# Strided attention on one core: normalisation spread over three engines, sums one group ahead, and stores of half the partitions

## The chip, the cores and the metric

The kernel runs on one core of a Trainium2 chip. The metric is the device time of one execution in microseconds (us). Seven executions of the kernel before gave a median of 129.85 us (129.51 to 129.98).

## What is computed

Attention in which every query looks at the same few keys: of the 1024 positions, those at 0, 64, 128, ..., 16 in all. Batch 8, heads 12, sequence 1024, head dimension 64, all float32.

```python
attend_positions = np.arange(0, seq, stride)
k = K[:, :, attend_positions, :]
v = V[:, :, attend_positions, :]
scores = np.einsum('bhqd,bhkd->bhqk', q, k) / np.sqrt(dim)
weights = np.exp(scores - np.max(scores, axis=-1, keepdims=True))
weights = weights / (np.sum(weights, axis=-1, keepdims=True) + 1e-10)
result[:, :, i, :] = np.einsum('bhqk,bhkd->bhqd', weights, v)[:, :, 0, :]
```

The output has the shape of Q. Q is 25.2 MB and so is the output; of K and V only one row in 64 is read.

## The kernel before

The 96 pairs of batch and head are taken in 24 groups of 4 (`HG`, `NG`). A group's queries fill one SBUF tile of 128 partitions by 2048 float32 numbers, 1 MB: each partition holds 32 consecutive rows of one head. In the output tile of a group a partition holds 16 consecutive rows of one head, and 16 of the head two further on. All DMAs are issued by SyncE (SP) on one queue, in the order of the program; each also waits until the eighth DMA before it on that queue has landed.

At the start K, V and the first ten groups of Q are loaded (`QBUFS = 10`), and constants are made: an identity, two permutations of it, a selector of the four heads (`s_sel`, and `slot_m` as float32), a mask for the values. `keys(m)` multiplies the keys of eight groups with the four head masks (L161, VectorE), spreads them with products on TensorE (L169) into a PSUM tile from the pool of the outputs, and copies them into `k_t` (L177, ScalarE). `value_rows` casts V and spreads it into `v_rep` by four products (L188) and four casts (L192).

A group then goes through these steps:

- `cast`: float32 to bfloat16 on GpSimd (L207)
- `transpose`: 32 by 32 blocks on VectorE (L211)
- `scores`: four accumulating products on TensorE into one PSUM bank (L218), then exp on ScalarE in two halves of 64 partitions (L229), into one of three weight tiles
- `values`: the value rows times the mask on GpSimd (L199)
- `sums`: eight small products with `s_sel` (L238), and a reciprocal on VectorE (L242)
- `outputs(g, c)` for c from 0 to 3: two products into a PSUM tile of one bank (L249), and the scaling with the reciprocals on VectorE (L254), into `out_sb`
- `store`: 1 MB to DRAM; a partition's 8 KB go out as two runs of 4 KB

The order on each engine is that of the program, since the schedule is written by hand (`manual_schedule`). In round g of the loop stand, in this order, the transpose of group g + 2, the sums of g, half of the outputs of g, the scores of g + 1, the other half of the outputs, the values of g + 2, the cast of g + 3, the store of g, and the load of g + 10. `keys` for later groups stands in rounds 2 and 4.

The output tiles are nine (`OBUFS = 9`), the PSUM pool of the outputs has four tiles of one bank.

Of the kernel before, what the change touches and what calls it, by code (L numbers as in the profile page):

```python
# [11 lines left out]
FP32 = mybir.dt.float32  # L12
BF16 = mybir.dt.bfloat16
I16 = mybir.dt.int16
I32 = mybir.dt.int32
AF = mybir.ActivationFunctionType
ALU = mybir.AluOpType


def _ap_with(ap: bass.AP, new_ap, extra_offset: int = 0) -> bass.AP:  # L20
    return dataclasses.replace(
        ap, ap=[list(p) for p in new_ap], offset=ap.offset + extra_offset
    )


def _copy(nc, out: bass.AP, in_: bass.AP):

    sides = [
        mybir.BassSymbolicTensorAccessPattern(
            ap=side.ap, dtype=side.dtype, bass_ap=side,  # L30
            is_dma=True, for_custom_bir_dma=True,
        )
        for side in (in_, out)
    ]
    return nc.sync.add_instruction(
        mybir.InstDMACopy(
            name=nc.get_next_instruction_name(), engine=mybir.EngineType.SP,
            ins=sides[:1], outs=sides[1:], queue="qSPDynamicHW",
            mode="Copy",
        )  # L40
    )
# [4 lines left out]

@with_exitstack
def kernel(  # L50
    ctx: ExitStack,
# [7 lines left out]
    nc = tc.nc  # L59

    B, H, S, D = Q.shape
    NK = S // stride
    scale = 1.0 / math.sqrt(D)

    P = 128
    HG = 4
    NG = B * H // HG
    NC = NG // 2
    SD = S * D
    KW = P + NK  # L70
    assert B * H == NG * HG and S == 1024 and D == 64 and NK == 16
    QBUFS = 10
    OBUFS = 9

    const = ctx.enter_context(tc.tile_pool(name="const", bufs=1))
    qn_pool = ctx.enter_context(tc.tile_pool(name="qn", bufs=QBUFS))
    out_pool = ctx.enter_context(tc.tile_pool(name="outsb", bufs=OBUFS))
# [2 lines left out]
    vb_pool = ctx.enter_context(tc.tile_pool(name="vb", bufs=3))  # L80
    rec_pool = ctx.enter_context(tc.tile_pool(name="rec", bufs=2))
    psum_sc = ctx.enter_context(tc.tile_pool(name="psc", bufs=2, space=bass.MemoryType.PSUM))
    psum_o = ctx.enter_context(tc.tile_pool(name="po", bufs=4, space=bass.MemoryType.PSUM))
    psum_s = ctx.enter_context(tc.tile_pool(name="psm", bufs=2, space=bass.MemoryType.PSUM))

    ctx.enter_context(tc.manual_schedule())
# [3 lines left out]
    v_raw = const.tile([P, NC, D], FP32, name="v_raw")  # L90
# [3 lines left out]
    def load(g):  # L94
        qn[g] = qn_pool.tile([P, 32 * D], FP32, name="qn", tag="qn")
        n = P if g < 2 else 32
        _copy(nc, qn[g], _ap_with(Q, [[HG * SD // n, n], [1, HG * SD // n]], g * HG * SD))
# [14 lines left out]
    perm_v = const.tile([P, 2, 2, 2, 2, NK], BF16, name="perm_v")  # L112
# [8 lines left out]
    for c in range(2):  # L121
        for a in range(2):
            for e in range(2):
                nc.gpsimd.tensor_copy(
                    out=perm_v[:, c, a, :, e], in_=id_v[:, c, :, a]
# [5 lines left out]
    for i in range(3):  # L131
# [7 lines left out]
        out=slot_i, in0=iota_p, scalar1=4, scalar2=3,  # L139
# [4 lines left out]
    s_sel = const.tile([P, 4], BF16, name="s_sel")  # L144
    nc.vector.tensor_scalar(  # L145
        out=s_sel, in0=col4, scalar1=slot_f, scalar2=None, op0=ALU.is_equal
    )
    slot_m = const.tile([P, 4], FP32, name="slot_m")
    nc.vector.tensor_copy(out=slot_m, in_=s_sel)
    mask = const.tile([P, 4, D], BF16, name="mask")  # L150
# [4 lines left out]
    v_rep = const.tile([P, NC, 2, D], BF16, name="v_rep")  # L155


    def keys(m):
        kr = k_raw[:, 4 * m : 4 * m + 4].rearrange("p n (q f) -> p n f q", f=2)
        for h in range(4):  # L160
            nc.vector.tensor_scalar(  # L161
                out=k_m[:, 4 * m : 4 * m + 4, :, h], in0=kr,
                scalar1=slot_m[:, h : h + 1], scalar2=None, op0=ALU.mult,
            )
        for u in range(2):
            kp = psum_o.tile([P, 2, 2, 2, 4 * NK], FP32, name="kp", tag="o")
            for i in range(2):
                for f in range(2):
                    nc.tensor.matmul(  # L169
                        kp[:, i, :, f],  # L170
                        lhsT=k_m[:, 4 * m + 2 * u + i, f].rearrange("p h q -> p (h q)"),
                        rhs=perm_k.rearrange("p c a b k -> p c (a b k)"),
                        start=True, stop=True,
                    )
            g0 = 8 * m + 4 * u
            dst = k_t[:, g0 : g0 + 4]
            nc.scalar.copy(  # L177
                _ap_with(dst, [dst.ap[0], [KW, 8], [32, 4], [1, NK]], extra_offset=NK),
                kp.rearrange("p i c f (s k) -> p (i c f) s k", s=4),
            )  # L180


    def value_rows():
        nc.vector.tensor_copy(out=v_bf, in_=v_raw)
        for n in range(2):
            for c in range(2):
                vp = psum_sc.tile([P, NC // 2, D], FP32, name="vp", tag="sc")
                nc.tensor.matmul(  # L188
                    vp, lhsT=perm_v[:, c].rearrange("p a b e k -> p (a b e k)"),
                    rhs=v_bf[:, 6 * n : 6 * n + 6], start=True, stop=True,  # L190
                )
                nc.vector.tensor_copy(out=v_rep[:, 6 * n : 6 * n + 6, c], in_=vp)  # L192

    qb, qt, wt, vb, rec, out_sb = {}, {}, {}, {}, {}, {}


    def values(g):
# [7 lines left out]
    def cast(g):  # L205
        qb[g] = qb_pool.tile([P, 32 * D], BF16, name="qb", tag="qb")
        nc.gpsimd.tensor_copy(out=qb[g], in_=qn[g])  # L207

    def transpose(g):
        qt[g] = qt_pool.tile([P, 32 * D], BF16, name="qt", tag="qt")  # L210
        nc.vector.transpose(qt[g].bitcast(I32), qb[g].bitcast(I32))  # L211

    def scores(g):
        sc = psum_sc.tile([P, 512], FP32, name="sc", tag="sc")
        q = qt[g]
        for e in range(2):
            for f in range(2):
                nc.tensor.matmul(  # L218
                    sc, lhsT=k_t[:, g, f, NK * (1 - e) : NK * (1 - e) + P],
                    rhs=_ap_with(  # L220
                        q, [q.ap[0], [2 * D, 8], [16 * D, 2], [2, 32]],
                        extra_offset=D * e + f,
                    ),
                    start=e + f == 0, stop=e + f == 2,
                )
        w = wt[g] = w_bufs[g % 3]
        for a in range(2):
            wa = w[64 * a : 64 * a + 64]
            nc.scalar.activation(  # L229
                out=_ap_with(wa, [wa.ap[0], [P, 8], [1, 2], [2, 32]], extra_offset=64 * a),  # L230
                in_=sc[64 * a : 64 * a + 64].rearrange("p (t x q) -> p t x q", t=8, x=2),
                func=AF.Exp, bias=0.0, scale=scale,
            )

    def sums(g):
        sm = psum_s.tile([P, 2, 8, 2], FP32, name="sm", tag="sm")
        for i in range(8):
            nc.tensor.matmul(  # L238
                sm[:, :, i], lhsT=wt[g][:, i], rhs=s_sel, start=True, stop=True
            )  # L240
        rec[g] = rec_pool.tile([P, 2, 16], FP32, name="rec", tag="rec")
        nc.vector.reciprocal(rec[g], sm.rearrange("p b i e -> p b (i e)"))  # L242

    def outputs(g, c):
        if c == 0:
            out_sb[g] = out_pool.tile([P, 2, 16, D], FP32, name="out_sb", tag="out_sb")
        ps = psum_o.tile([P, 2, 2, 2 * D], FP32, name="o_ps", tag="o")
        for i in range(2):
            nc.tensor.matmul(  # L249
                ps[:, :, i], lhsT=wt[g][:, 2 * c + i],  # L250
                rhs=vb[g].rearrange("p s d -> p (s d)"),
                start=True, stop=True,
            )
        nc.vector.tensor_tensor(  # L254
            out=out_sb[g][:, :, 4 * c : 4 * c + 4],
            in0=ps.rearrange("p b i (e d) -> p b (i e) d", e=2),
            in1=rec[g][:, :, 4 * c : 4 * c + 4].unsqueeze(3).to_broadcast([P, 2, 4, D]),
            op=ALU.mult,
        )

    def store(g):
        o = out_sb[g]
        _copy(
            nc,
            _ap_with(out, [[16 * D, P], [2 * SD, 2], [1, 16 * D]], g * HG * SD),
            _ap_with(o, [o.ap[0], [1, 1], [1, 32 * D]]),
        )

    keys(0)
    cast(0)  # L270
    transpose(0)
    scores(0)
    value_rows()
    values(0)
    cast(1)
    transpose(1)
    values(1)
    cast(2)
    for g in range(NG):
        if g + 2 < NG:  # L280
            transpose(g + 2)
        sums(g)
        outputs(g, 0)
        outputs(g, 1)
        if g + 1 < NG:
            scores(g + 1)
        outputs(g, 2)
        outputs(g, 3)
        if g + 2 < NG:
            values(g + 2)  # L290
        if g + 3 < NG:
            cast(g + 3)
        if g in (2, 4):
            keys(g // 2)
        store(g)
        if g + QBUFS < NG:
            load(g + QBUFS)


# [1 line left out]
_INS = ['Q', 'K', 'V', 'stride']  # L301
_OUTS = [((8, 12, 1024, 64), 'float32')]
# [30 lines left out]
```

The softmax here doesn't subtract the row's maximum and nothing guards it: scores larger than these inputs give would overflow.

## Time and profile before

One execution was profiled:

| What | Value |
|---|---|
| Time of the profiled execution | 129.78 us |
| Its span, first to last instruction | 128.0 us |
| VectorE (DVE) busy | 109.2 us, 85% |
| GpSimd (POOL) busy | 66.6 us, 52% |
| TensorE (PE) busy | 74.4 us, 58% |
| ScalarE (ACT) busy | 39.6 us, 31% |
| Mean DMA rate over the span | 400 GB/s |
| First store issued | 23.57 us |
| Second store issued | 27.55 us |
| Last store issued | 120.1 us |

The profile is read so: a slice is a fortieth of the span, and a digit in it is the busy share in tenths. A group of instructions has its busy time, its count and the mean time of one. The DMA share is the mean busy share of the sixteen DMA engines of the core. Durations of one instruction can overlap with the next on the same engine: a run of four L254 takes 2.48 us where one has 0.68.

### The profile page before, as it was taken

How to read it: one execution, taken by the hardware profiler on the slowest of the kernel's cores; microseconds unless marked ns; L12 is line 12 of the kernel's file. 1: busy time of each engine (PE TensorE's matmuls, PEld its weight loads, DVE VectorE, ACT ScalarE, POOL GpSimd, SP SyncE). 2: the span in 40 equal slices, each digit the busy share in tenths (PEclk: the TensorE clock that was granted, in tenths of full speed). 3: DMA queues.
4: the chain of work that ended last, by engine and by line, in shares of the span. 5: the costliest groups of instructions: out<-in, count | busy, mean ns of one | idle time of the engine just before them, and what ended most of it. 6: DMA issues, size and time to landing. Idle time of an engine off the chain costs nothing. (4 is left out here: it accounts for less than half of the span.)

```text
span 128.0 us, 1518 instructions
## 1 busy us (share of the span) xinstructions
PE 74.4 (58%) x508; PEld 39.2 (31%) x508; DVE 109.2 (85%) x170; ACT 39.6 (31%) x55; POOL 66.6 (52%) x69
## 2 busy tenths in 40 slices
PE   0007767974486097866675579776567579674000
PEld 0003233441433064333342234333334333332000
DVE  6996458999969986899999999999999999999500
ACT  3003404224234234344423440444442343432000
POOL 8971499675217605387767644738765743100000
PEclk9999999999769855599999965579999955999655
DMA  2999989898998998989989999999999999999980
GB/s 69 356 315 479 461 369 481 369 451 351 479 458 343 494 404 379 509 366 415 499 335 448 433 402 440 438 397 448 438 394 453 402 425 420 422 425 422 425 353 41
DMA packets 7913, 51.23 MB, mean 400 GB/s; under 512 B 3872, under 2 KB 3872, under 8 KB 3872
## 3 DMA queue, kind: packets, MB, share of 16 engines
q1 hardware_dynamic: 7904, 51.12, 96.4%
q8 instruction: 4, 0.07, 0.2%
q14 instruction: 5, 0.04, 0.1%
HBM read 25.95 MB, written 25.17 MB: 399 GB/s over the span
## 5 line engine op out<-in xcount | busy, mean ns | idle before, releaser
L254 DVE TENSOR_TENSOR out_sb<-o_ps,rec 128x512 f32<-128x512 f32 x96 | 59.9, 684 | 5.0 <-PE o_ps L249 2.7
L229 ACT ACTIVATE w<-sc 64x512 bf16<-64x512 f32 x48 | 35.1, 731 | 60.3 <-PE sc L218 57.5
L207 POOL CAST qb<-qn 128x2048 bf16<-128x2048 f32 x24 | 45.5, 1897 | 0.9 <-DMA qn<-in_Q_dram 0.9
L249 PE MATMUL o_ps<-vb,w 128*128 128x256 bf16 x192 | 38.1, 327 | 1.8 <-DVE out_sb L254 1.0
L199 POOL TENSOR_TENSOR vb<-mask,v_rep 128x256 bf16<-128x256 bf16 x24 | 16.1, 669 | 41.1 <-PE o_ps L249 36.8
L218 PE MATMUL sc<-qt,k_t 128*128 128x512 bf16 x96 | 33.9, 487 | 1.4 <-DVE qt L211 1.2
L211 DVE STREAM_TRANSPOSE qt<-qb 128x1024 int32<-128x1024 int32 x24 | 29.6, 1235 | 1.6 <-POOL qb L207 1.6
L249 PEld LDWEIGHTS <-w 128*128 128x128 bf16 x192 | 19.7, 112 | 15.6 <-issue 8.2
L238 PE MATMUL sm<-s_sel,w 128*128 128x4 bf16 x192 | 8.7, 167 | 21.8 <-ACT w L229 21.8
L238 PEld LDWEIGHTS <-w 128*128 128x128 bf16 x192 | 7.0, 101 | 29.9 <-ACT w L229 29.3
L218 PEld LDWEIGHTS <-k_t 128*128 128x128 bf16 x96 | 11.1, 117 | 12.4 <-issue 7.1
L169 PE MATMUL kp<-perm_k,k_m 128*128 128x128 bf16 x24 | 3.1, 311 | 17.4 <-DVE k_m L161 17.4
L242 DVE RECIPROCAL rec<-sm 128x32 f32<-128x32 f32 x24 | 7.8, 326 | 0.3 <-PE sm L238 0.3
L169 PEld LDWEIGHTS <-k_m 128*128 128x128 bf16 x24 | 2.3, 140 | 18.2 <-DVE k_m L161 18.2
L177 ACT CAST k_t<-kp 128x512 bf16<-128x512 f32 x6 | 3.2, 589 | 14.1 <-PE kp L169 14.1
L161 DVE TENSOR_SCALAR k_m<-k_raw,slot_m 128x256 bf16<-128x256 f32 x12 | 6.8, 626 | 0.0
L192 DVE CAST v_rep<-vp 128x384 bf16<-128x384 f32 x4 | 2.2, 558 | 2.6 <-PE vp L188 2.6
L135 POOL MEMSET k_t<- 128x4608 bf16 x1 | 3.9, 3940 | 0.0
L145 DVE TENSOR_SCALAR s_sel<-col,slot_f 128x4 bf16<-128x4 int16 x1 | 3.1, 3145 | 0.1
L188 PE MATMUL vp<-v_bf,perm_v 128*128 128x384 bf16 x4 | 2.0, 489 | 0.8 <-DVE v_rep L192 0.6
L177 ACT ACT_TABLE_LOAD x1 | 1.3, 1283 | 2.1 <-DVE k_t L129 2.1
L129 DVE MEMSET k_t<- 128x1152 uint32 x1 | 1.0, 1018 | 1.0 <-PEq L314 1.0
(17 smaller groups left out, 6.2 us busy)
## 6 DMA issues: line engine op xcount, KB each, us to landing
qn<-in_Q_dram SPq DMA_DIRECT2D x24, 1024.0 KB, 13.8
out_dram<-out_sb SPq DMA_DIRECT2D x24, 1024.0 KB, 11.9
k_raw<-in_K_dram SPq DMA_DIRECT2D x1, 384.0 KB, 4.5
v_raw<-in_V_dram SPq DMA_DIRECT2D x1, 384.0 KB, 7.6
```

Of the source, the lines that this page charges most:

```text
L161: nc.vector.tensor_scalar(out=k_m[:, 4 * m : 4 * m + 4, :, h], in0=kr, scalar1=slot_m[:, h : h + 1], scalar2=None, op0=ALU.mult,)
L169: nc.tensor.matmul(kp[:, i, :, f], lhsT=k_m[:, 4 * m + 2 * u + i, f].rearrange("p h q -> p (h q)"), rhs=perm_k.rearrange("p c a b k -> p c ...
L177: nc.scalar.copy(_ap_with(dst, [dst.ap[0], [KW, 8], [32, 4], [1, NK]], extra_offset=NK), kp.rearrange("p i c f (s k) -> p (i c f) s k", s=4),)
L199: nc.gpsimd.tensor_tensor(out=vb[g], in0=mask, in1=v_rep[:, g // 2, g % 2].unsqueeze(1).to_broadcast([P, 4, D]), op=ALU.mult,)
L207: nc.gpsimd.tensor_copy(out=qb[g], in_=qn[g])
L211: nc.vector.transpose(qt[g].bitcast(I32), qb[g].bitcast(I32))
L218: nc.tensor.matmul(sc, lhsT=k_t[:, g, f, NK * (1 - e) : NK * (1 - e) + P], rhs=_ap_with(q, [q.ap[0], [2 * D, 8], [16 * D, 2], [2, 32]], ex ...
L229: nc.scalar.activation(out=_ap_with(wa, [wa.ap[0], [P, 8], [1, 2], [2, 32]], extra_offset=64 * a), in_=sc[64 * a : 64 * a + 64].rearrange( ...
L238: nc.tensor.matmul(sm[:, :, i], lhsT=wt[g][:, i], rhs=s_sel, start=True, stop=True)
L242: nc.vector.reciprocal(rec[g], sm.rearrange("p b i e -> p b (i e)"))
L249: nc.tensor.matmul(ps[:, :, i], lhsT=wt[g][:, 2 * c + i], rhs=vb[g].rearrange("p s d -> p (s d)"), start=True, stop=True,)
L254: nc.vector.tensor_tensor(out=out_sb[g][:, :, 4 * c : 4 * c + 4], in0=ps.rearrange("p b i (e d) -> p b (i e) d", e=2), in1=rec[g][:, :, 4 ...
```

## The change

The steps of a group are the same, but they are cut and ordered differently.

- `OBUFS` goes from 9 tiles of one group (8 KB in a partition) to 4 tiles of two groups (16 KB). The PSUM pool of the outputs goes from four tiles of one bank to two of two banks.
- `keys` is split. `key_rows` does the masking, on ScalarE in place of VectorE, in rounds 1 and 5; the products and copies follow in rounds 2 and 6, into PSUM tiles of the scores.
- `value_rows` is split in two, the second half in round 3, into PSUM tiles of the sums. The cast of V stands alone before the scores of group 0.
- The casts of groups 0 and 1 stand at the start; the transpose of group 1 follows the scores of group 0.
- The query positions of a group are laid out in another order (the access pattern in `scores`), so that a head's rows lie together in the output tile.
- `sums` is split. `sums_mm` forms the sums with the selector as the stationary side and the weights as the moving side, four products of 32 rows; `sums_rec` transposes them from PSUM in 32 by 32 blocks and takes reciprocals. Both are done for group g + 1 in round g.
- `outputs` keeps only products, four into one PSUM tile; `normalize` scales. Of the two halves, the first is scaled by VectorE in one instruction of 1024 elements; of the second, VectorE scales 512 elements, and the other 512 are copied by ScalarE and scaled in SBUF by GpSimd.
- The scores of g + 1 come before all outputs of g.
- `store(n, h)` stores half the partitions (64) of two groups, 16 KB a partition in four runs of 4 KB. After every second group two such stores are issued, each followed by a load.

```diff
-    OBUFS = 9
+    OBUFS = 4
...
-    psum_o = ctx.enter_context(tc.tile_pool(name="po", bufs=4, space=bass.MemoryType.PSUM))
+    psum_o = ctx.enter_context(tc.tile_pool(name="po", bufs=2, space=bass.MemoryType.PSUM))
...
+    sel32 = const.tile([P, 32], BF16, name="sel32")
+    nc.vector.memset(sel32, 0.0)
+    nc.vector.tensor_copy(out=sel32[:, 0:4], in_=s_sel)
...
-    def keys(m):
+    def key_rows(m):
         kr = k_raw[:, 4 * m : 4 * m + 4].rearrange("p n (q f) -> p n f q", f=2)
         for h in range(4):
-            nc.vector.tensor_scalar(
-                out=k_m[:, 4 * m : 4 * m + 4, :, h], in0=kr,
-                scalar1=slot_m[:, h : h + 1], scalar2=None, op0=ALU.mult,
-            )
+            nc.scalar.activation(
+                out=k_m[:, 4 * m : 4 * m + 4, :, h], in_=kr,
+                func=AF.Copy, scale=slot_m[:, h : h + 1],
+            )
+
+    def keys(m):
         for u in range(2):
-            kp = psum_o.tile([P, 2, 2, 2, 4 * NK], FP32, name="kp", tag="o")
+            kp = psum_sc.tile([P, 2, 2, 2, 4 * NK], FP32, name="kp", tag="sc")
...
-    def value_rows():
-        nc.vector.tensor_copy(out=v_bf, in_=v_raw)
-        for n in range(2):
-            for c in range(2):
-                vp = psum_sc.tile([P, NC // 2, D], FP32, name="vp", tag="sc")
+    def value_rows(n):
+        for c in range(2):
+            vp = psum_s.tile([P, NC // 2, D], FP32, name="vp", tag="sm")
...
-                        q, [q.ap[0], [2 * D, 8], [16 * D, 2], [2, 32]],
-                        extra_offset=D * e + f,
+                        q, [q.ap[0], [D, 8], [16 * D, 2], [2, 32]],
+                        extra_offset=8 * D * e + f,
...
-    def sums(g):
-        sm = psum_s.tile([P, 2, 8, 2], FP32, name="sm", tag="sm")
-        for i in range(8):
+    def sums_mm(g):
+        sm = sm_ps[g] = psum_s.tile([P, 8, 32], FP32, name="sm", tag="sm")
+        for q in range(4):
             nc.tensor.matmul(
-                sm[:, :, i], lhsT=wt[g][:, i], rhs=s_sel, start=True, stop=True
-            )
-        rec[g] = rec_pool.tile([P, 2, 16], FP32, name="rec", tag="rec")
-        nc.vector.reciprocal(rec[g], sm.rearrange("p b i e -> p b (i e)"))
+                sm[32 * q : 32 * q + 32], lhsT=sel32,
+                rhs=wt[g][:, :, 32 * q : 32 * q + 32],
+                start=True, stop=True, tile_position=(0, 32 * q),
+            )
+
+    def sums_rec(g):
+        sm = sm_ps[g]
+        smt = rec_pool.tile([P, 8, 32], FP32, name="smt", tag="smt")
+        nc.vector.transpose(
+            smt.rearrange("p i r -> p (i r)"), sm.rearrange("p i r -> p (i r)")
+        )
+        rec[g] = rec_pool.tile([P, 8, 4], FP32, name="rec", tag="rec")
+        nc.vector.reciprocal(rec[g], smt[:, :, 0:4])
 
     def outputs(g, c):
         if c == 0:
-            out_sb[g] = out_pool.tile([P, 2, 16, D], FP32, name="out_sb", tag="out_sb")
-        ps = psum_o.tile([P, 2, 2, 2 * D], FP32, name="o_ps", tag="o")
-        for i in range(2):
+            if g % 2 == 0:
+                out_2[g // 2] = out_pool.tile(
+                    [P, 2, 4, 8, D], FP32, name="out_sb", tag="out_sb"
+                )
+            out_sb[g] = out_2[g // 2][:, g % 2]
+        ps = psum_o.tile([P, 4, 4, D], FP32, name="o_ps", tag="o")
+        o_ps[g, c] = ps
+        for i in range(4):
             nc.tensor.matmul(
-                ps[:, :, i], lhsT=wt[g][:, 2 * c + i],
+                ps[:, i].rearrange("p s d -> p (s d)"), lhsT=wt[g][:, 4 * c + i],
                 rhs=vb[g].rearrange("p s d -> p (s d)"),
                 start=True, stop=True,
             )
+
+    def normalize(g, c):
+        ps = o_ps[g, c]
+        i0 = 4 * c
+        n = 4 if c == 0 else 2
+        part = lambda k, m: out_sb[g][:, :, k : k + m].rearrange("p s i d -> p i s d")
+        fact = lambda k, m: rec[g][:, k : k + m].unsqueeze(3).to_broadcast([P, m, 4, D])
+        if n < 4:
+            nc.scalar.copy(part(i0 + n, 4 - n), ps[:, n:4])
         nc.vector.tensor_tensor(
-            out=out_sb[g][:, :, 4 * c : 4 * c + 4],
-            in0=ps.rearrange("p b i (e d) -> p b (i e) d", e=2),
-            in1=rec[g][:, :, 4 * c : 4 * c + 4].unsqueeze(3).to_broadcast([P, 2, 4, D]),
-            op=ALU.mult,
-        )
-
-    def store(g):
-        o = out_sb[g]
+            out=part(i0, n), in0=ps[:, 0:n], in1=fact(i0, n), op=ALU.mult
+        )
+        if n < 4:
+            nc.gpsimd.tensor_tensor(
+                out=part(i0 + n, 4 - n), in0=part(i0 + n, 4 - n),
+                in1=fact(i0 + n, 4 - n), op=ALU.mult,
+            )
+
+    def store(n, h):
+        o = out_2[n][64 * h : 64 * h + 64]
         _copy(
             nc,
-            _ap_with(out, [[16 * D, P], [2 * SD, 2], [1, 16 * D]], g * HG * SD),
-            _ap_with(o, [o.ap[0], [1, 1], [1, 32 * D]]),
-        )
-
+            _ap_with(
+                out, [[16 * D, 64], [2 * SD, 4], [1, 16 * D]],
+                2 * n * HG * SD + h * SD,
+            ),
+            _ap_with(o, [o.ap[0], [1, 1], [1, 64 * D]]),
+        )
+
+    key_rows(0)
+    cast(0)
+    cast(1)
+    transpose(0)
     keys(0)
-    cast(0)
-    transpose(0)
+    nc.vector.tensor_copy(out=v_bf, in_=v_raw)
     scores(0)
-    value_rows()
+    transpose(1)
+    value_rows(0)
     values(0)
-    cast(1)
-    transpose(1)
     values(1)
     cast(2)
+    sums_mm(0)
+    sums_rec(0)
     for g in range(NG):
         if g + 2 < NG:
             transpose(g + 2)
-        sums(g)
+        if g + 1 < NG:
+            scores(g + 1)
         outputs(g, 0)
         outputs(g, 1)
         if g + 1 < NG:
-            scores(g + 1)
-        outputs(g, 2)
-        outputs(g, 3)
+            sums_mm(g + 1)
         if g + 2 < NG:
             values(g + 2)
         if g + 3 < NG:
             cast(g + 3)
-        if g in (2, 4):
-            keys(g // 2)
-        store(g)
-        if g + QBUFS < NG:
-            load(g + QBUFS)
+        normalize(g, 0)
+        normalize(g, 1)
+        if g + 1 < NG:
+            sums_rec(g + 1)
+        if g in (1, 5):
+            key_rows(g // 4 + 1)
+        if g in (2, 6):
+            keys(g // 4 + 1)
+        if g == 3:
+            value_rows(1)
+        if g % 2 == 1:
+            for h in range(2):
+                store(g // 2, h)
+                if g - 1 + h + QBUFS < NG:
+                    load(g - 1 + h + QBUFS)
```

## The prediction

> **What bounds the kernel now.** I read the page's slices first, then its queue table, its chain, its groups, and then asked for the busy time in stretches.
>
> From the page, parts 2 to 4 and 6:
>
> ```profile
> DMA  2999989898998998989989999999999999999980
> q1 hardware_dynamic: 7904, 51.12, 96.4%
> HBM read 25.95 MB, written 25.17 MB: 399 GB/s over the span
> ...
> DVE out_sb L254 1%; DVEq L328 0%; DVE rec L242 0%
> ...
> qn<-in_Q_dram SPq DMA_DIRECT2D x24, 1024.0 KB, 13.8
> out_dram<-out_sb SPq DMA_DIRECT2D x24, 1024.0 KB, 11.9
> ```
>
> The DMA digits stand at 8 or 9 from the second slice to the last but one, and the packets took 96.4% of sixteen engines' span: 123.4 of 128.0 us. The chain names VectorE, but holds only a few per cent of the span, so it doesn't say what bounds. A transfer of 1 MB lands 12 to 14 us after its issue, five times the 2.5 us that 1.05 MB needs at 425 GB/s: transfers stand in line.
>
> From the busy time by stretch (stretch, length, busy us and instructions of PE, PEld, DVE, ACT, POOL, then clock, DMA share, GB/s):
>
> ```profile
> 0.00:4.00 4.00, 0.00 (x0) 0.00 (x0) 2.64 (x6) 1.28 (x1) 3.40 (x21) 1.00 0.42 98
> 12.00:20.00 8.00, 5.98 (x25) 2.27 (x24) 3.98 (x6) 1.47 (x3) 5.54 (x6) 1.00 1.05 442
> 20.00:28.00 8.00, 6.53 (x39) 3.30 (x38) 7.79 (x13) 2.94 (x4) 6.71 (x6) 1.00 0.95 397
> ...
> 56.00:84.00 28.00, 19.46 (x142) 10.30 (x141) 27.34 (x44) 10.23 (x14) 18.05 (x15) 0.83 1.03 434
> ...
> 112.00:120.00 8.00, 3.69 (x36) 2.17 (x36) 7.82 (x14) 2.05 (x3) 0.00 (x0) 0.94 1.01 422
> 120.00:124.00 4.00, 0.00 (x0) 0.00 (x0) 0.11 (x1) 0.00 (x0) 0.00 (x0) 0.50 0.99 416
> 124.00:126.00 2.00, 0.00 (x0) 0.00 (x0) 0.00 (x0) 0.00 (x0) 0.00 (x0) 0.50 0.34 143
> ```
>
> The DMA engines are full from 4 to 124 us, at about 425 GB/s, with loads alone, with both kinds, and with stores alone after 104. VectorE is nearly full too (27.34 of 28 us) but ends at 120.1, with some 4 us of transfers left. So the bound is bytes over DMA rate: 51.12 MB at 425 GB/s is 120 us, after a start of 3 and before a tail of 4. VectorE is second by about 2 us.
>
> The groups that the change touches:
>
> ```profile
> L254 DVE TENSOR_TENSOR out_sb<-o_ps,rec 128x512 f32<-128x512 f32 x96 | 59.9, 684 | 5.0 <-PE o_ps L249 2.7
> L229 ACT ACTIVATE w<-sc 64x512 bf16<-64x512 f32 x48 | 35.1, 731 | 60.3 <-PE sc L218 57.5
> L207 POOL CAST qb<-qn 128x2048 bf16<-128x2048 f32 x24 | 45.5, 1897 | 0.9 <-DMA qn<-in_Q_dram 0.9
> L199 POOL TENSOR_TENSOR vb<-mask,v_rep 128x256 bf16<-128x256 bf16 x24 | 16.1, 669 | 41.1 <-PE o_ps L249 36.8
> L211 DVE STREAM_TRANSPOSE qt<-qb 128x1024 int32<-128x1024 int32 x24 | 29.6, 1235 | 1.6 <-POOL qb L207 1.6
> L242 DVE RECIPROCAL rec<-sm 128x32 f32<-128x32 f32 x24 | 7.8, 326 | 0.3 <-PE sm L238 0.3
> L177 ACT CAST k_t<-kp 128x512 bf16<-128x512 f32 x6 | 3.2, 589 | 14.1 <-PE kp L169 14.1
> L161 DVE TENSOR_SCALAR k_m<-k_raw,slot_m 128x256 bf16<-128x256 f32 x12 | 6.8, 626 | 0.0
> ```
>
> [...]
>
> **The change part by part.**
>
> *Scaling on three engines, sums by transpose.* Before, VectorE has per group 1235 + 4 × 684 + 326 = 4.30 us by durations; back to back it runs a group in about 3.97 (15.64 busy in 16 us holds four). After: transpose 1235; one scaling of 1024 elements, estimated from 512 at 684 ns and a slope of 1 ns an element, 1.19; one of 512, 684; a transpose of 256 from PSUM, estimated from 1235 less 768 elements, 0.47; reciprocal 326. Sum 3.91, so 0.39 less: a pitch near 3.6. GpSimd gets 512 elements of float32:[...] L199's 669 for half as many gives 1.3; I take 1.2. Its group becomes 1.90 + 0.67 + 1.2 = 3.8. ScalarE: 2 × 731 and a copy of 512 near 589, 2.1. No engine passes the DMA's pace, 2.1 MB a group or 4.9 us. Gain on the time: nothing, since the transfers cover it; without that cover it would be 24 × 0.39 = 9 us.
>
> *Key masks to ScalarE, key products in the score banks, values in two steps.* VectorE loses 12 × 626 = 7.5 us (two runs of 2.8 lie in the loop), ScalarE gains 12 of 0.4 to 0.7 us and has 60 us of idle time. In the loop keys now wait for a score bank, 1 to 2 us twice; again beside transfers. Nothing either way.
>
> *Early second cast and transpose.* Groups 0 and 1 end earlier: the cast of group 1 no longer stands behind the value product (at 15.07 us before, after a wait of 4.4). The first store leaves later than now (23.57), as it needs both groups; I put it at 26 to 27, about where group 1's store is now (27.55). The ten first loads are 11.3 MB with keys and values; summing the stretches they keep the engines to 30 us or so. So no hole, unless the first pair is later than 29; each us beyond that would cost one.
>
> *Sums one group ahead.* The sums now wait for exp of g+1 on TensorE; behind them stand the scores of g+2, which the next sums need. A round is 1.9 of scores, 1.7 of exp beside outputs, 0.5 of sums: about 4.1, under 4.9.
>
> *The stores.* Same 24, same 1.05 MB, but each from 64 partitions of 16 KB where it was 128 of 8 KB. Per-packet cost can fall: between nothing and 1 us in all. [...] The tail between 124 and 126 us at a share of 0.34 shows that engines do finish apart, by some 2 us of 120. [...] 24 × 2.1 = 51 us. All of it lies on the path, since nothing else sets the end.
>
> Sum against the profiled execution: 129.78 (128.0 of span) + 51 = 181; it stands 0.07 below the median 129.85.
>
> **The rivals.**
>
> A (forecast): [...] 172 to 188, likeliest 181. For: the bound is DMA, nothing covers it. Against: no half-width transfer is in this trace.
>
> B: [...] engines drift apart, as the tail hints; penalty 10 to 42 us, 140 to 172, about 157.
>
> C, the other side: the half-width stores run at full rate[...]. Then bytes are the same, the larger packets save up to 1 us, no hole opens: 129.0, range 128.6 to 129.6. Decisive point: a store costs no more than 2.46 us of the engines' time. That VectorE's saving shows as 9 us is excluded by the DMA share.
>
> D: stores are full rate, but the new hand-offs between engines bring a group's round to 4.5 us, so the last pair leaves at 27 + 22 × 4.5 = 126 and its 2 MB land 7 us later: 133 to 136. Up to 4.2 us a round it would not show. For: exp, sums, their transpose, the copy on ScalarE and the scaling on GpSimd now follow each other across engines within a round; against: the sums for TensorE and GpSimd above.
>
> **How the numbers follow.** A 0.53, B 0.24, C 0.17, D 0.06. The time is A's, 181. The range leaves out C and what is above A: 131 to 189; A's own is 172 to 188. A measurement here can tell about 0.2%, 0.26 us, from no change. Faster takes most of C, 0.15; within 0.2% the rest of it, 0.02; slower 0.83.
>
> **What would show it.** If A: DMA digits still 9, but GB/s near 290 where loads and stores mix (2.1 MB in 2.46 + 4.6 us) and near 225 where only stores are left; 4.6 us between landings of stores; compute idle, waiting for free output tiles. If B, the rate climbs along the run. If C: over 420 GB/s throughout and a first store before 29 us. If D: DMA digits under 9 after the first third. VectorE's row for 1024 elements near 1.2 us, GpSimd's scaling near 1.2, and a VectorE share well under 85% would bear out the compute sums. I am wrong altogether if the rate of stores alone is above 400 GB/s.

## The result and the profile after

The changed kernel took 137.77 us (median of 12 runs), the kernel before 129.82. Its own runs lie between 134.2 and 143.3: the three nearest its fastest (134.2 to 135.4), which alone count for the ratio, are 3.8% slower than the kernel before (1.038, 95% interval 1.035 to 1.041), the medians differ by 6.1%, and the execution that was profiled is among the slower ones. It took 138.7 us, 136.6 of them in the span.

From its page, parts 2 to 4 and 6:

```profile
span 136.6 us, 1401 instructions
...
DMA  3999899989899998999999999999999999999950
...
q1 hardware_dynamic: 6368, 51.12, 95.3%
...
HBM read 25.95 MB, written 25.17 MB: 374 GB/s over the span
...
DMA 54%; POOL 14%; issue 8%; DVE 6%; PE 3%; SPq 3%; DVEq 1%; ACT 0%; POOLq 0%
...
qn<-in_Q_dram SPq DMA_DIRECT2D x24, 1024.0 KB, 19.7
out_dram<-out_sb SPq DMA_DIRECT2D x24, 1024.0 KB, 19.6
```

The DMA engines are as full as before, with the same 51.12 MB in fewer packets, yet they move 374 GB/s where it was 399. The chain of waits now follows transfers: half of the span is the wait for them. A busy digit here says that packets are under way, not that they go at full speed: below, a share of 1.00 goes with 367 GB/s.

The busy time by stretch says when the speed was missing (stretch, length, busy us and instructions of PE, PEld, DVE, ACT, POOL, then clock, DMA share, GB/s):

```profile
20.00:32.00 12.00, 8.81 (x57) 4.42 (x58) 11.76 (x17) 8.82 (x15) 12.00 (x11) 1.00 0.95 397
32.00:56.00 24.00, 19.13 (x111) 9.42 (x111) 22.21 (x33) 15.12 (x25) 21.51 (x20) 0.93 1.00 367
56.00:84.00 28.00, 17.98 (x92) 8.51 (x91) 20.30 (x30) 12.24 (x18) 17.68 (x16) 0.75 1.00 403
84.00:100.00 16.00, 10.77 (x49) 5.00 (x49) 11.36 (x17) 6.18 (x9) 10.92 (x10) 0.71 1.00 426
112.00:120.00 8.00, 5.57 (x29) 2.63 (x28) 6.15 (x9) 2.77 (x5) 4.70 (x5) 0.63 1.01 408
120.00:128.00 8.00, 0.00 (x0) 0.00 (x0) 1.96 (x3) 0.59 (x1) 1.04 (x1) 0.58 1.01 343
128.00:136.00 8.00, 0.00 (x0) 0.00 (x0) 0.00 (x0) 0.00 (x0) 0.00 (x0) 0.50 0.45 170
```

Before the first store moves at about 30 us nothing is different (393 GB/s from 20 to 28 us, 397 before). The rate drops with the first stores, climbs for 50 us by itself, is whole between 84 and 100, and drops again at the end. In the kernel before, the stretch of the drop ran at 427 GB/s, at a DMA share of 1.01:

```profile
32.00:56.00 24.00, 15.99 (x111) 9.21 (x112) 20.54 (x34) 7.99 (x12) 10.15 (x9) 0.72 1.01 427
```

The trace shows something else beside the rate, from the signals with which each of the sixteen engines reports its part of a transfer. They finish a transfer within 0.5 us of each other at 31 us, within 3 us at 45, within 9.4 us from 91 to 111. They drift apart as the rate recovers. A packet of 16 KB took 0.61 to 0.62 us when undisturbed and up to 1.5 in the slow stretches; a load's packet of 32 KB up to 2.5 instead of 1.21.

The new operations, by shape:

```profile
L282 DVE TENSOR_TENSOR out_sb<-o_ps,rec 128x1024 f32<-128x1024 f32 x24 | 28.6, 1190 | 1.4 <-PE o_ps L268 0.9 <-DVE rec L255 0.5
L286 POOL TENSOR_TENSOR out_sb<-out_sb,rec 128x512 f32<-128x512 f32 x24 | 25.0, 1042 | 6.5 <-ACT out_sb L281 6.5
L282 DVE TENSOR_TENSOR out_sb<-o_ps,rec 128x512 f32<-128x512 f32 x24 | 16.2, 676 | 0.4 <-ACT out_sb L281 0.3
L281 ACT COPY out_sb<-o_ps 128x512 f32<-128x512 f32 x24 | 14.1, 586 | 9.3 <-DMA out_dram<-out_sb 6.9 <-PE o_ps L268 1.7 <-issue 0.2
```

They cost about what was estimated. Of the 9.3 us that ScalarE stood idle before its copies, 6.9 were waits for output tiles whose stores hadn't landed.

### The profile page after: what moved, and what is told of

The parts are those of the page before. It is cut to its first block, busy times and chain, and to the rows that moved or that the text cites. A ratio compares the mean times of both kernels' runs of the same rounds, so it can differ in the third digit from the quotient of the medians.

```text
span 136.6 us, 1401 instructions
## 1 busy us (share of the span) xinstructions
PE 78.8 (58%) x412; PEld 37.5 (27%) x412; DVE 95.3 (70%) x136; ACT 58.8 (43%) x91; POOL 90.5 (66%) x93
## 3 DMA queue, kind: packets, MB, share of 16 engines
q1 hardware_dynamic: 6368, 51.12, 95.3%
## 4 chain that ended last, share of the span: by engine, by line
DMA 54%; POOL 14%; issue 8%; DVE 6%; PE 3%; SPq 3%; DVEq 1%; ACT 0%; POOLq 0%
DMA out_dram<-out_sb 47%; DMA qn<-in_Q_dram 7%; POOL qb L211 6%; POOL out_sb L286 5%; POOL vb L203 3%; DVE qt L215 3%; DVE out_sb L282 3%; PE sc L222 2%; SPq L35 2%; PE o_ps L268 1%; DVEq L373 0%; ACT out_sb L281 0%; SPq L102 0%; DVE v_rep L196 0%; SPq L100 0%
## 5 line engine op out<-in xcount | busy, mean ns | idle before, releaser
L282 DVE TENSOR_TENSOR out_sb<-o_ps,rec 128x1024 f32<-128x1024 f32 (+1 forms) x48 | 43.1, 933 | 1.8 <-PE o_ps L268 0.9
L268 PE MATMUL o_ps<-vb,w 128*128 128x256 bf16 x192 | 34.3, 326 | 1.2 <-DVE out_sb L282 0.6
L286 POOL TENSOR_TENSOR out_sb<-out_sb,rec 128x512 f32<-128x512 f32 x24 | 25.0, 1042 | 6.5 <-ACT out_sb L281 6.5
L268 PEld LDWEIGHTS <-w 128*128 128x128 bf16 x192 | 21.2, 116 | 19.2 <-DVE out_sb L282 8.8
L281 ACT COPY out_sb<-o_ps 128x512 f32<-128x512 f32 x24 | 14.1, 586 | 9.3 <-DMA out_dram<-out_sb 6.9
L242 PE MATMUL sm<-w,sel 128*32 128x256 bf16 x96 | 12.1, 311 | 6.0 <-ACT w L233 3.8
L255 DVE RECIPROCAL rec<-smt 128x32 f32<-128x32 f32 x24 | 8.5, 353 | 2.7 <-POOL vb L203 0.5
L251 DVE STREAM_TRANSPOSE smt<-sm 128x256 f32<-128x256 f32 x24 | 10.3, 428 | 0.0
L242 PEld LDWEIGHTS <-sel 128*32 128x32 bf16 x96 | 4.3, 95 | 15.7 <-issue 12.9
L165 ACT ACTIVATE k_m<-k_raw,slot_m 128x256 bf16<-128x256 f32 x12 | 5.3, 515 | 1.1 <-DVE slot_m L153 1.1
```

Of the source, the lines that this page charges most:

```text
L242: nc.tensor.matmul(sm[32 * q : 32 * q + 32], lhsT=sel32, rhs=wt[g][:, :, 32 * q : 32 * q + 32], start=True, stop=True, tile_position=(0, 3 ...
L251: nc.vector.transpose(smt.rearrange("p i r -> p (i r)"), sm.rearrange("p i r -> p (i r)"))
L255: nc.vector.reciprocal(rec[g], smt[:, :, 0:4])
L268: nc.tensor.matmul(ps[:, i].rearrange("p s d -> p (s d)"), lhsT=wt[g][:, 4 * c + i], rhs=vb[g].rearrange("p s d -> p (s d)"), start=True, ...
L281: nc.scalar.copy(part(i0 + n, 4 - n), ps[:, n:4])
L282: nc.vector.tensor_tensor(out=part(i0, n), in0=ps[:, 0:n], in1=fact(i0, n), op=ALU.mult)
```

## The experiments

### Full-width stores in the changed kernel

The first replaces a pair's two half-width stores by one of 2 MB, issued before the pair's two loads:

```diff
-    def store(n, h):
-        o = out_2[n][64 * h : 64 * h + 64]
+    def store(n):
+        o = out_2[n]
...
-            _ap_with(
-                out, [[16 * D, 64], [2 * SD, 4], [1, 16 * D]],
-                2 * n * HG * SD + h * SD,
-            ),
+            _ap_with(out, [[16 * D, P], [2 * SD, 4], [1, 16 * D]], 2 * n * HG * SD),
```

> The changed kernel, with the two half-width stores of a pair of groups replaced by one store of 2 MB from all 128 partitions (16 KB each, the same four runs of 4 KB in DRAM). Theory H (half the partitions): [...] 128.5 to 129.8 us, rate above 415 GB/s from 8 us to the end, landings of one transfer within 3 us of each other. Theory P (16 KB pieces or their four runs in DRAM are what slows transfers): still 134 or more. Theory C (new hand-offs between engines or the later first store): still 134 or more.

The second keeps 24 stores of 1 MB at the same places, each of one group and all partitions:

```diff
-        o = out_2[n][64 * h : 64 * h + 64]
+        o = out_2[n][:, h]
...
-                out, [[16 * D, 64], [2 * SD, 4], [1, 16 * D]],
-                2 * n * HG * SD + h * SD,
+                out, [[16 * D, P], [2 * SD, 2], [1, 16 * D]],
+                (2 * n + h) * HG * SD,
...
-            _ap_with(o, [o.ap[0], [1, 1], [1, 64 * D]]),
+            _ap_with(o, [o.ap[0], [1, 1], [1, 32 * D]]),
```

> The changed kernel, with each store taking one group from all 128 partitions (8 KB each, two runs of 4 KB, as before the change), at the same places in the order. Theory H: 128.8 to 130 us, as before the change. Theory P: 129 to 130 too. Theory C: 134 or more. With the full-width pair store it tells H from P: under H both are fast, under P only this one.

Measured: 129.76 us for the first (1.0014 of before, 0.9994 to 1.0035) and 129.40 for the second, which is faster than the kernel before by a quarter of a per cent (0.9976, 0.9963 to 0.9989; 129.71 beside it). Stretches of the second:

```profile
32.00:56.00 24.00, 18.69 (x119) 9.58 (x119) 22.89 (x35) 16.05 (x26) 22.60 (x21) 1.00 1.01 427
56.00:84.00 28.00, 19.81 (x117) 9.16 (x117) 24.99 (x36) 15.41 (x23) 22.32 (x19) 1.00 1.02 432
84.00:100.00 16.00, 11.15 (x48) 5.19 (x48) 12.21 (x17) 6.17 (x9) 11.88 (x12) 0.56 0.99 418
112.00:120.00 8.00, 0.00 (x0) 0.00 (x0) 0.44 (x1) 0.00 (x0) 0.00 (x0) 0.59 1.01 425
```

Theory H holds as far as the half of the partitions goes: neither the 16 KB pieces nor the new hand-offs cost anything that these times show. Both versions keep the four output tiles of two groups, so these aren't the cause either. The last stretch shows what the compute parts bring: the engines are done some 8 us earlier than before (0.44 us of VectorE after 112 us; it ended at 120.1), and the time hardly moves. The second version is the fastest of the three, by little.

### The stores alone in the kernel before

```diff
-    OBUFS = 9
+    OBUFS = 4
...
-            out_sb[g] = out_pool.tile([P, 2, 16, D], FP32, name="out_sb", tag="out_sb")
+            if g % 2 == 0:
+                out_2[g // 2] = out_pool.tile(
+                    [P, 2, 2, 16, D], FP32, name="out_sb", tag="out_sb"
+                )
+            out_sb[g] = out_2[g // 2][:, g % 2]
```

with `store(n, h)` and its place as in the changed kernel.

> The kernel before, with nothing changed but its output tiles (four of two groups) and its stores (half the partitions of two groups, as in the changed kernel). Theories H and P: the whole loss is there, 133 to 142 us, with the rate under 410 GB/s between 32 and 56 us. Theory C: 129.5 to 131.

Measured: 137.77 us (137.2 to 143.5; ratio 1.062, 1.057 to 1.067), with 361 GB/s between 32 and 56 us. The whole loss is there with the stores alone.

### The DRAM side made contiguous

```diff
-                out, [[16 * D, 64], [2 * SD, 4], [1, 16 * D]],
-                2 * n * HG * SD + h * SD,
+                out, [[64 * D, 64], [16 * D, 4], [1, 16 * D]],
+                2 * n * HG * SD + h * HG * SD,
```

> The changed kernel, but a half-width store puts the 16 KB of a partition in one contiguous run of DRAM and the next partition behind it, so rows of the output stand in other places than the reference has them. Theory H (SBUF side): still 133 to 142 us. If instead the DRAM side is what collides (four runs 512 KB apart from each of sixteen engines): 128.5 to 130.

Measured: 138.37 us (136.3 to 140.5; ratio 1.058, 1.050 to 1.066). The four runs in DRAM aren't the cause; the half of the partitions is what is left.

### Stores without anything beside them

In these kernels only transfers are left. Against Theory H1 stands what the prediction took, about half the rate for every store. The store is the changed kernel's; `o` is one of four tiles set to 1 at the start. The full-width control and the lower half differ from it in the source:

```diff
+    for n in range(NG // 2):
+        for h in range(2):
+            store(n, h)
...
-        o = out_2[n % OBUFS][64 * h : 64 * h + 64]
+        o = out_2[n % OBUFS][0:64]
```

> No compute and no loads: four output tiles are set to 1 and the 24 half-width stores, lower and upper half in turn, are issued one after the other (the output is all ones). The step of my prediction[...]: 4.8 us between landings, [...] 16 KB packets of 1.2 us. Theory H1, that only a store beside another engine's load collides: 2.46 us between landings, over 415 GB/s, packets of 0.62 us.

> As the one before, with all 24 stores read from partitions 0 to 63 (the output is all ones). [...] Theory H1: over 415 GB/s.

> No compute and no loads: 24 full-width stores of one group (128 partitions, 8 KB each), issued one after the other (the output is all ones). The control for the half-width stores alone. If half-width sharing alone explains those: 2.46 us between landings from the first store on, no wide spread, about 70 us. If stores alone are slow for another reason, the first ten stores are slow here too, 78 us or more.

Measured: full width 69.77 us, halves in turn 80.77, lower half always 132.35. One stretch of the full width, as the control (stretch, length, VectorE, GpSimd, clock, DMA share, GB/s):

```profile
8.00:20.00 12.00, 8.34 (x3) 0.00 (x0) 1.00 1.02 420
```

Then the halves in turn, and below them the lower half:

```profile
8.00:20.00 12.00, 8.34 (x3) 0.00 (x0) 1.00 0.94 223
20.00:32.00 12.00, 0.00 (x0) 0.00 (x0) 1.00 1.01 328
32.00:44.00 12.00, 0.00 (x0) 0.00 (x0) 1.00 0.99 412
44.00:60.00 16.00, 0.00 (x0) 0.00 (x0) 1.00 1.01 426
```

```profile
8.00:20.00 12.00, 8.34 (x3) 0.00 (x0) 1.00 0.95 197
20.00:32.00 12.00, 0.00 (x0) 0.00 (x0) 1.00 1.04 216
32.00:44.00 12.00, 0.00 (x0) 0.00 (x0) 1.00 0.96 199
44.00:60.00 16.00, 0.00 (x0) 0.00 (x0) 1.00 1.01 208
```

Both start at about half of the control's rate (223 and 197 GB/s against 420), with packets of 1.27 us. With the lower half it stays so, 5.12 us from landing to landing. With the halves in turn the engines' completions of one store lie 0.2 us apart for the first, 3.3 for the fifth and 5.4 to 5.5 from the ninth on, and from then the rate is whole (426 GB/s from 44 to 60 us). Which half an engine reads at a moment the trace doesn't say. Stores alone are enough for the loss, so Theory H1, that only a store beside a load collides, was wrong.

### Loads and half-width stores without compute

Here the ten first loads are issued, and then each store is followed by a load, as in the changed kernel.

```diff
+    for g in range(QBUFS):
+        load(g)
     for n in range(NG // 2):
         for h in range(2):
             store(n, h)
+            if 2 * n + h + QBUFS < NG:
+                load(2 * n + h + QBUFS)
```

> No compute: the 24 loads of Q and the 24 half-width stores in the changed kernel's order, without K and V and with no waits on compute (the output is all ones). Theory H1: the first store at full rate, then packets of 1 to 2.5 us once loads and stores run on different engines at the same time, a rate under 410 GB/s for some 20 us, and landings of one transfer spread over 5 us or more. If compute has a part in it: above 418 GB/s throughout.

> No compute: 24 loads and 24 stores in the changed kernel's order, all stores read from partitions 0 to 63 (the output is all ones). If engines stay in step, as my prediction took it, each store costs 5.07 us as in the run with the lower half alone: near 185 us. If loads let partners fall out of step,[...] the collisions fade as they did with the halves in turn: 130 to 140 us.

Measured: 133.52 us (131.6 and 135.5) and 158.74. Stretches of the one with the lower half always:

```profile
28.00:56.00 28.00, 0.00 (x0) 0.00 (x0) 1.00 1.01 372
56.00:84.00 28.00, 0.00 (x0) 0.00 (x0) 1.00 0.99 378
84.00:104.00 20.00, 0.00 (x0) 0.00 (x0) 1.00 0.97 398
108.00:124.00 16.00, 0.00 (x0) 0.00 (x0) 1.00 1.02 217
```

While loads stand between the stores, the rate rises slowly, and the completions of one transfer go from 0.4 to 7 us apart; when the loads are over, at about 107 us, every transfer left is a store of the lower half and the rate falls at once (217 GB/s). With both halves in turn it was 376, 408, 424 and 424 in the same stretches. The loss needs no compute. The time of 158.74 lies between the two values expected: with loads between the stores most of the loss is gone (372 to 398 GB/s), at the end it is not.

### Every second partition

A store again takes 64 partitions, but 0, 2, 4, ... or 1, 3, 5, .... Theory H1 says here that it matters which 64 partitions a store takes:

```diff
-        o = out_2[n][64 * h : 64 * h + 64]
+        o = out_2[n]
...
-                out, [[16 * D, 64], [2 * SD, 4], [1, 16 * D]],
-                2 * n * HG * SD + h * SD,
+                out, [[2 * 16 * D, 64], [2 * SD, 4], [1, 16 * D]],
+                2 * n * HG * SD + h * 16 * D,
...
-            _ap_with(o, [o.ap[0], [1, 1], [1, 64 * D]]),
+            _ap_with(
+                o, [[2 * o.ap[0][0], 64], [1, 1], [1, 64 * D]], h * o.ap[0][0]
+            ),
```

> The changed kernel, but a store takes every second partition (0, 2, 4, ... or 1, 3, 5, ...) instead of the lower or upper half: again 64 partitions, 16 KB each, four runs of 4 KB, 24 stores. Theory H1[...]: 128.8 to 130.5 us. Theory H2 (64 partitions are bad however they are chosen): 133 to 143 us.

Measured: 135.86 us (ratio 1.042, 1.035 to 1.050). That spoke against the choice of partitions as the cause. But the edit had changed the DRAM side too: only every second row of 4 KB is written. Three more kernels took the two apart: the even partitions alone, into neighbouring rows; the same into every second row; and the whole kernel with every second partition but neighbouring rows.

The source and the two DRAM sides; in the stores alone the offset of the source is left at 0:

```diff
-        o = out_2[n % OBUFS][64 * h : 64 * h + 64]
+        o = out_2[n % OBUFS]
...
-            _ap_with(o, [o.ap[0], [1, 1], [1, 64 * D]]),
+            _ap_with(o, [[2 * o.ap[0][0], 64], [1, 1], [1, 64 * D]]),
```

```python
out, [[16 * D, 64], [2 * SD, 4], [1, 16 * D]], 2 * n * HG * SD + h * SD          # neighbouring rows
out, [[2 * 16 * D, 64], [2 * SD, 4], [1, 16 * D]], 2 * n * HG * SD + h * 16 * D  # every second row
```

> No compute and no loads: 24 stores, all read from partitions 0, 2, 4, ... 126 (the output is all ones). [...] 2.46 us between landings, about 70 us. [...] slow at first, and then full rate once engines have moved apart, 75 to 85 us; 132 us if they never do.

> Stores alone from partitions 0, 2, 4, ..., now into every second row of 4 KB in DRAM (even rows and odd rows in turn; the output is all ones). If the steps of 8 KB in DRAM cost time by themselves: over 72 us, packets above 0.65 us. If they cost only beside loads, or nothing: 69 us as before.

> The kernel with stores of every second partition, but with the DRAM side of the changed kernel: the 64 partitions go to 64 neighbouring rows of 4 KB, so rows of the output stand in other places than the reference has them. If [...] the steps of 8 KB in DRAM were what slowed every second partition: 128.8 to 130.2 us. If 64 partitions beside loads are slow however they lie and wherever they go: 133 to 138 us.

Measured: 68.86, 72.53 and 129.36 us (ratio of the last 0.9988, 0.9974 to 1.0003). The even partitions alone run at the full rate from the start:

```profile
8.00:20.00 12.00, 8.34 (x3) 0.00 (x0) 1.00 0.99 415
```

The slow start, which one theory of that run expected, isn't there. The whole kernel's stretches have no hole:

```profile
32.00:56.00 24.00, 18.86 (x114) 9.70 (x114) 22.73 (x34) 15.62 (x25) 21.78 (x20) 0.93 1.01 425
56.00:84.00 28.00, 20.30 (x120) 9.39 (x120) 25.71 (x38) 15.87 (x24) 23.59 (x21) 1.00 1.01 429
84.00:100.00 16.00, 10.10 (x49) 4.75 (x49) 11.91 (x17) 6.17 (x9) 11.48 (x11) 0.79 1.00 425
```

So 64 partitions are no fault in themselves: spread over both halves they are as fast as 128 (68.86 us against 69.77 alone, 129.36 against 129.40 in the whole kernel). This kernel differs from the changed one only in which partitions a store takes. It writes the same addresses in DRAM, so rows of the output stand in other places than in the reference. The 135.86 of every second partition came with the 8 KB steps in DRAM, which the changed kernel doesn't have. How they cost was not looked into; there too the completions drift apart, from 0.5 us at 31 to 6.3 at 113.

## Why the prediction was wrong

**What bounds the kernel: right.** The DMA engines before and after are full from 4 us on (a share of 1.08 and 1.06 from 4 to 12 us, 1.01 and 1.00 from 32 to 56). In the version with full-width group stores compute ends 8 us earlier, and that changed the time by 0.3 us.

**The compute parts: right.** VectorE's scaling of 1024 elements took 1190 ns where 1.19 us was estimated, GpSimd's 1042 ns where I took 1.2 us, ScalarE's copy 586 where I took 589 ns, the transpose of sums 428 ns where 0.47 us was estimated, a key mask on ScalarE 515 ns where I took 0.4 to 0.7 us. The slope of 1 ns an element behind the first and the fourth was an estimate too; the groups after give (1190 − 676) / 512 = 1.0. GpSimd is the fullest engine between 20 and 32 us (12.00 of 12.00 us), at 3.46 us a group, under the DMA's 4.9. The first store left at 25.59 us (26 to 27 predicted), and no hole opened. Rival D is out.

**The half rate of one half: right, and nearly in size.** That a store from one half runs at about half the rate, I took so; no trace before the change has such a store. The lower half alone gives 1.05 MB in 5.12 us, 205 GB/s, where full width gave 416 to 420. The runs show the rate, not its cause. The 2.1 us a store more that I charged are 2.6 in the measurement ((132.35 − 69.77) / 24).

**The step that failed** is the product 24 × 2.1 = 51 us: I let the offset between engines, a quarter us by my estimate, stand still, and so charged 24 stores alike. In the runs the offset grows. With halves in turn and nothing else, the price of a store falls to nothing as it does, and the whole loss is 11.0 us (80.77 − 69.77), all of it in the first ten stores, instead of 24 × 2.6 = 62. In the changed kernel it is 8 us by the medians and 5 by the ratio of 1.038. Between its profile and that of the full-width group stores, 9.0 us of span: 1.4 MB missing from 32 to 56 us at 427 GB/s is 3.4 us, 0.8 MB from 56 to 84 is 1.9, and the rest, 3.7, comes after 112 us, when only stores are left, the rate drops again (343 GB/s at a DMA share of 1.01 from 120 to 128) and engines finish apart (share 0.45 in the last 8).

The signs that the prediction had named say the same. The rate climbs along the run (367, 403, 426 GB/s), the sign of rival B, and from 112 to 120 us, with only stores left, it is 408, over the 400 that was to show it wrong altogether; the 290 and 225 of the forecast didn't come. That 137.77 lies in the range from 131 to 189 is luck, since the range was wide enough for B and D: it is below what the forecast (172 to 188) and B (140 to 172) gave for themselves, and beside D's 133 to 136 by another cause.

My rival B had this, engines that drift apart, and the tail of the profile before had hinted at it (a share of 0.34 from 124 to 126 us). I gave it the smaller chance and too high a price (10 to 42 us), because I took it that stores from opposite halves hold each other up all along, which no trace before showed. The runs show that for the first stores only, 223 GB/s with the halves in turn against 197 with the lower half; ten stores later the halves in turn moved 426 GB/s. I should have asked what becomes of the offset once an engine is ahead: in the halves in turn it grew from 0.2 us to 5.5 and stayed there.

**What stays open.** That the drift ends the loss rests on the two going together; no run held the engines in step. Why an engine gets ahead was not traced to single engines. In the halves in turn the sixteen completions of a store pair up 2.46 us, one store, apart, but only to within 0.35 us. In the changed kernel two thirds of the first store's packets, behind loads, took 0.62 us though all engines were in it together (its completions lie 0.33 us apart), and only the last of them up to 1.5 us, while in the stores alone the first packets took 1.13 to 1.28; no run shows why. Why the rate drops again in the last stores was not tried. The scatter of the changed kernel's runs (134 to 143 us) fits a drift that goes differently each time: it is there in every version that mixes loads with stores of the lower and the upper half, and missing in stores alone (132.35 and 132.36 for the lower half, 80.73 and 80.81 for the halves in turn) and at full width (129.1 to 130.5). That is an inference.

## What to carry to other kernels

Where a kernel is bound by DMA, look at the rate, not at the DMA share: here the share was 1.00 at 367 GB/s and 1.01 at 427. Cut stores so that each takes all partitions, or partitions spread evenly over both halves (every second one here, with the rows in DRAM next to each other), and don't split by lower and upper half (here 129.40 and 129.36 us against 137.77). When you price such a loss, ask whether the engines drift apart under it and it fades: in stores alone it was 11 us where 24 equal losses would have been 62, though in the changed kernel some of it came back in the last stores.

## What the runs showed of the hardware

- Two kinds of 64-partition store: partitions 0 to 63, 205 GB/s; partitions 0, 2, ..., 126, 415 to 436 GB/s from the first store on, 0.9 us less in all than 128 partitions of 8 KB (68.86 against 69.77 us); the prediction gave the larger packets between nothing and 1 us.
- Writing every second 4 KB row of DRAM cost stores alone 3.7 us of 69 (72.53 against 68.86), but 6.5 us beside loads (135.86 against 129.36), with 351 GB/s between 32 and 56 us.
- Engines 9 us apart at the same transfer don't slow the queue as such: the changed kernel moved 426 GB/s so. They cost at the end, when the last engines finish alone (170 GB/s at a share of 0.45 from 128 to 136 us).
